# A transformer block on one core: the first 512 gate columns of the up projection are taken from rows without rstd and shift

## The chip, the cores and the metric

The kernel runs on one core of a Trainium2 chip. The metric is the device time of one execution in microseconds; before the change its median is 1419.35 us in three runs (1419.31 to 1419.57).

## What is computed

One layer of a diffusion backbone in fp32: 256 latent tokens and 256 context tokens of width D = 2048, neighbourhood attention (16 heads of 128), then a gated feed-forward part with a short convolution along the tokens (FFN_DIM 5504). Shift, scale and gate of both parts come from SiLU(c) @ w_ada. The part that the change touches:

```python
def rms_norm(x, g):
    y = x32 * lax.rsqrt(jnp.mean(x32 * x32, axis=-1, keepdims=True) + EPS)
    return (y * g).astype(x.dtype)

def modulate(x, shift, scale):
    return x * (1.0 + scale) + shift

def conv_ffn(h, w_up, conv_w, conv_b, w_down):
    gate, up = jnp.split(dwconv3(h @ w_up, conv_w, conv_b), 2, axis=-1)
    return (jax.nn.silu(gate) * up) @ w_down

x = x + g1 * y                                   # y: attention @ w_o
hf = modulate(rms_norm(x, norm_ffn_g[i]), sh2, sc2)
x = x + g2 * conv_ffn(hf, ...)
```

With gs2 = norm_ffn_g (1 + sc2), a row of hf is x gs2 rstd + sh2, where rstd is one number for each token.

## The kernel before

**Layout.** Features lie on the 128 partitions and tokens along a row, so x1 (the residual stream) is 16 row tiles (index kt or db) of 128 features by T = 256 tokens. The kernel has one long order of products on PE: the projection of q, k and v with the attention beside it, w_o, w_up, w_down.

**Split operands.** Each fp32 operand is split in two fp32r parts: hi, a rounded copy, and lo, the rest. A weight tile (128 rows by 2 row tiles by up to 512 columns) is loaded by `wload` on the SP queue into one of four wr buffers; `wpair` copies hi to wh on ACT (three buffers) and subtracts for lo on DVE into wl (two buffers, L158). A plan lists all tiles in order, and `ahead` keeps two split pairs ahead of use. The moving operand has hi and lo side by side: a row of 2T = 512 columns.

**`proj` (L709)** runs one piece of columns over all row tiles, two row tiles to a step: for each block of 128 columns and each row tile wh by the 512 columns (hi and lo; L723), then wl by the 256 hi columns (L729). At the end, columns 0 to 255 of a bank plus columns 256 to 511 are the result. With `fold` the 512 columns are taken as two products of 256 into the same bank columns, which need no addition later; the last piece of w_o (256 output features) is done so.

**The stage with w_o.** The table WO cuts the 2048 outputs into pieces: 768 in two halves of k, then 512, 512 and 256. After a piece each of its blocks db is added to x1 (L775, two operations, one if folded), squared on ACT for the sum over features (L780, added up by DVE in sacc2, L784), and multiplied by gs2 into `xg` on ACT (L785). Beside these products DVE accumulates the vectors g1, gs2 and sh2 from w_ada (L274), which `ada.tick` hands out after each step; `ada.drain` after the last but one piece finishes them (transposes on PE L282, reduction and addition on DVE L285, L288).

**Between w_o and w_up.** The squares of the last two blocks and sacc2 are summed over the partitions by six products with a column of ones (`col_sums`, L229). `rstd_rows` makes rstd of them (POOL power, three small DVE operations), a diagonal matrix (L215) and one product with ones (L220) that spreads rstd over all partitions; ACT copies it to rb2 (L222). Then for each row tile t = xg rb2 (on DVE, from the fourth on every second one on POOL), hf hi = t + sh2 (ACT, L814) and hf lo (DVE, L815). `hold` makes the weight splits that are emitted next wait for the last square and the diagonal.

**The stage with w_up.** The 5504 gate and 5504 up columns go in pieces of 512, gate and up in turn, so that a first pass takes gate columns 0 to 511 and a second the up columns 0 to 511. Beside a pass the finished four blocks of the pass before are handled in `side`: `drop` adds the two halves of a bank (L824, L825), `conv` the three taps, then `gate` or `up`.

**Order of the work.** The kernel is written engine-neutral; a scheduler with its own estimate of time puts each engine's instructions in an order. PE, DVE, ACT, POOL and SP each work through theirs.

## Time and profile before

| | |
|---|---|
| median of three runs | 1419.35 us (1419.31 to 1419.57) |
| the profiled execution | 1419.36 us |
| its span, first to last instruction | 1417.6 us |
| mean granted clock of PE | 0.996 |
| PE busy | 1386.8 us, 98% |
| DVE busy | 1022.4 us, 72% |
| ACT busy | 694.9 us, 49% |
| DMA | 317.13 MB, mean 224 GB/s |

All durations of the text come from the one profiled execution; its time is 0.01 us above the median. Between the span and the time lie 1.76 us of start and end. PE's matmuls are pipelined and their recorded ends are modelled, so a busy PE is best read by the distance of starts. A step's rhythm is such a distance.

### The profile page before, as it was taken

The page shows a single profiled execution, that of the slowest core. Times are in us where ns is not written, and L with a number is a line of the kernel's source. Part 1 is how long each engine was busy: PE and PEld are TensorE (multiplying, and loading weights), DVE is VectorE, ACT ScalarE, POOL GpSimd, SP SyncE. Part 2 cuts the span into 40 slices and gives each one's busy share as a digit, 9 for nine tenths or more (in the row PEclk, how much of TensorE's full clock was granted, in tenths as well). Part 3 has the DMA queues.
Part 4 walks back from the last instruction along what each step waited for, and adds up shares of the span by engine and source line. Part 5 has one row for each costly group of instructions (what it writes and reads, how often), then busy time and mean ns, then how long its engine had stood idle before and what let it go on. Part 6 is the DMA issues. An engine that isn't in the chain of part 4 may idle for free.

```text
span 1417.6 us, 20783 instructions
## 1 busy us (share of the span) xinstructions
PE 1386.8 (98%) x7608; PEld 1164.8 (82%) x7608; DVE 1022.4 (72%) x1669; ACT 694.9 (49%) x1212; POOL 59.9 (4%) x64
## 2 busy tenths in 40 slices
PE   4999999999999999999899999999999999999998
PEld 2566788888888888888788888888888888888888
DVE  4555678878877888788777888778787675545454
ACT  4322254564454564554565655556555554333343
POOL 1000010020010020000100000000000000000000
PEclk9999999999999999999899999999999999999999
DMA  9999637768776869475667777777776666666554
GB/s 304 357 353 292 223 104 237 227 214 257 233 238 192 276 201 291 157 250 178 225 187 237 237 236 238 225 237 235 231 230 189 175 192 197 188 200 201 169 181 154
DMA packets 208918, 317.13 MB, mean 224 GB/s; under 512 B 23360, under 2 KB 87744, under 8 KB 208816
## 3 DMA queue, kind: packets, MB, share of 16 engines
q1 hardware_dynamic: 208688, 315.79, 71.5%
q8 instruction: 59, 0.97, 0.3%
q14 instruction: 43, 0.35, 0.1%
q10 hardware_dynamic: 128, 0.01, 0.0%
HBM read 312.75 MB, written 3.01 MB: 223 GB/s over the span
## 4 chain that ended last, share of the span: by engine, by line
PE 94%; DMA 2%; DVE 2%; SPq 1%; ACT 1%; issue 1%; POOL 0%; DVEq 0%; ACTq 0%; POOLq 0%
PE pj L723 20%; PE pj L729 10%; PE mx L723 10%; PE pj L372 8%; PE pj L373 8%; PE pj L374 8%; PE ms L723 7%; PE mx L729 5%; PE ms L729 4%; PE mx L372 2%; PE mx L373 2%; PE ms L407 2%; PE mx L374 2%; DMA wx<-in_w_ada 1%; PE ms L627 1%; SPq L401 1%
## 5 line engine op out<-in xcount | busy, mean ns | idle before, releaser
L158 DVE TENSOR_TENSOR wl<-wr,wh 128x1024 fp32r<-128x1024 f32 (+2 forms) x425 | 478.1, 1126 | 284.8 <-PE pj L729 102.3
L157 ACT CAST wh<-wr 128x1024 fp32r<-128x1024 f32 (+2 forms) x425 | 412.6, 972 | 535.3 <-PE pj L723 164.3
L373 PE MATMUL pj<-wl,hh 128*128 128x512 f32 x512 | 202.7, 396 | 0.0
L374 PE MATMUL pj<-wh,hl 128*128 128x512 f32 x512 | 200.1, 393 | 0.0
L372 PE MATMUL pj<-wh,hh 128*128 128x512 f32 x512 | 193.0, 396 | 2.5 <-ACT hh L446 2.5
L274 DVE SCALAR_TENSOR_TENSOR acc<-wa,sT,acc 128x512 f32<-128x512 f32 x240 | 183.2, 765 | 2.5
L723 PE MATMUL pj<-hf,wh 128*128 128x512 f32 x688 | 176.1, 395 | 2.0 <-DVE hf L815 2.0
L723 PEld LDWEIGHTS pj<-hf,wh 128*128 128x128 f32 x688 | 124.6, 190 | 25.1 <-DVE hf L815 2.8
L372 PEld LDWEIGHTS pj<-wh,hh 128*128 128x128 f32 x512 | 95.7, 188 | 26.4 <-issue 3.4
L373 PEld LDWEIGHTS pj<-wl,hh 128*128 128x128 f32 x512 | 96.5, 188 | 21.5 <-DVE wl L158 0.9
L374 PEld LDWEIGHTS pj<-wh,hl 128*128 128x128 f32 x512 | 96.5, 188 | 18.8
L729 PEld LDWEIGHTS pj<-hf,wl 128*128 128x128 f32 x688 | 93.7, 190 | 6.7
L723 PE MATMUL mx<-hf,wh 128*128 128x512 f32 x352 | 97.7, 394 | 0.0
L729 PE MATMUL pj<-hf,wl 128*128 128x256 f32 x688 | 96.9, 283 | 0.0
L723 PE MATMUL ms<-hf,wh 128*128 128x512 f32 x336 | 90.9, 390 | 0.0
L723 PEld LDWEIGHTS ms<-hf,wh 128*128 128x128 f32 x336 | 63.1, 188 | 14.2
L474 DVE TENSOR_TENSOR vsum<-vsum,mx 128x512 f32<-128x512 f32 x64 | 43.1, 682 | 34.3 <-PE mx L374 34.1
L723 PEld LDWEIGHTS mx<-hf,wh 128*128 128x128 f32 x352 | 60.6, 190 | 7.8
L729 PEld LDWEIGHTS mx<-hf,wl 128*128 128x128 f32 x352 | 53.7, 189 | 6.8
L729 PE MATMUL mx<-hf,wl 128*128 128x256 f32 x352 | 55.9, 282 | 0.0
L729 PE MATMUL ms<-hf,wl 128*128 128x256 f32 x336 | 54.7, 283 | 0.0
L407 PE MATMUL ms<-wx,s 128*32 128x512 f32 (+1 forms) x288 | 36.9, 582 | 16.3 <-DMA wx<-in_w_ada 16.3
(248 smaller groups left out, 2029.6 us busy)
## 6 DMA issues: line engine op xcount, KB each, us to landing
wr<-in_w_up SPq DMA_DIRECT2D x160, 512.0 KB, 4.2
wa<-in_w_ada SPq DMA_DIRECT2D x128, 512.0 KB, 4.8
wr<-in_w_qkv SPq DMA_DIRECT2D x93, 512.0 KB, 4.2
wr<-in_w_down SPq DMA_DIRECT2D x63, 512.0 KB, 4.6
wx<-in_w_ada SPq DMA_DIRECT2D x56, 512.0 KB, 8.6
wr<-in_w_o SPq DMA_DIRECT2D x24, 512.0 KB, 5.0
wr<-in_w_down SPq DMA_DIRECT2D x45, 256.0 KB, 3.1
wr<-in_w_up SPq DMA_DIRECT2D x16, 384.0 KB, 3.4
```

Of the source, the lines that this page charges most:

```text
L157: a = nc.scalar.copy(hi[:, :kn, :cn], w[:, :kn, :cn])
L158: b = nc.vector.tensor_tensor(out=lo[:, :kn, :cn], in0=w[:, :kn, :cn], in1=hi[:, :kn, :cn].bitcast(F32), op=ALU.subtract,)
L274: nc.vector.scalar_tensor_tensor(out=acc, in0=w[:, k, :], scalar=s, in1=acc, op0=ALU.mult, op1=ALU.add)
L372: nc.tensor.matmul(pt, hh[:, kt, ts], wh[:, k, :], start=a, stop=False)
L373: nc.tensor.matmul(pt, hh[:, kt, ts], wl[:, k, :], start=False, stop=False)
L374: nc.tensor.matmul(pt, hl(kt, ts), wh[:, k, :], start=False, stop=z)
L401: load = nc.sync.dma_start(w.rearrange("p (k s f) -> p k s f", k=4, s=2)[:, :, which, :], w_ada[q * CH : (q + 1) * CH, c0 : c0 + n // 2].r ...
L407: nc.tensor.matmul(ap_[32 * k : 32 * k + 32, :n], s32[:, 4 * q + k, :], w[:, k * n : (k + 1) * n], start=(q == 0), stop=(q == 3), tile_pos ...
L474: nc.vector.tensor_add(acc[:, h0 + i, :], acc[:, h0 + i, :], pr_[i])
L627: nc.tensor.transpose(tp[:, kt * P : (kt + 1) * P], pr[:, kt * P : (kt + 1) * P], ident)
L723: nc.tensor.matmul(pts[b][:, : t1 - t0], wh[:, k, bs], mov(kt, slice(t0, t1)), start=(kt == 0 and t0 == 0), stop=False,)
L729: nc.tensor.matmul(pts[b][:, :T], wl[:, k, bs], mov(kt, slice(0, T)), start=False, stop=(kt == kn - 1),)
```

## The change

`proj` and its callers stay, but for the first gate piece the moving operand is another. The block's row x1 gs2 is itself split: ACT writes its hi part and a new DVE operation (L798 of the changed kernel) its lo part into `xgs`, two tiles of eight row tiles each, in rows of T + 2 = 258 columns; the last two columns hold sh2, also split. The first pass is run folded on these rows: per block and row tile three products of 258 columns (wh by hi, wh by lo, wl by hi). A bank then holds W x gs2 in 256 columns and W sh2 in the last two. `drop_late` finishes it: columns times rb2, plus the column of W sh2 as a bias. The 16 normalizations (`normalized`, now from x1, all on DVE and ACT) are handed out in `side` beside this first pass. `hold` goes. `act` creates its tiles when first used, since xgs lies in memory that they take later.

```diff
     def wpair(src, k0, kn, c0, cn):
...
-        with ExitStack() as order:
-            for ins in hold:
-                order.enter_context(tc.issue_after(ins))
-            a = nc.scalar.copy(hi[:, :kn, :cn], w[:, :kn, :cn])
...
             for b, bs, k in cells:
                 kt = k0 + k
-                for t0, t1 in ((0, T), (T, 2 * T)) if fold else ((0, 2 * T),):
+                for t in (slice(0, T), slice(T, 2 * T)) if fold else (slice(0, 2 * T),):
+                    m = mov(kt, t)
                     nc.tensor.matmul(
-                        pts[b][:, : t1 - t0], wh[:, k, bs], mov(kt, slice(t0, t1)),
-                        start=(kt == 0 and t0 == 0), stop=False,
+                        pts[b][:, : m.shape[-1]], wh[:, k, bs], m,
+                        start=(kt == 0 and t.start == 0), stop=False,
                     )
...
-    xg = big.tile([P, KD, T], F32, tag="row0", name="xg")
+    xgs = [
+        pool.tile([P, 8, 2, T + 2], F32R, tag=tag, name=f"xg_{tag}")
+        for pool, tag in ((big, "row1"), (hp, "hl1"))
+    ]
+
+    def xg(kt, part):
+        return xgs[kt // 8][:, kt % 8, part, :]
+
...
             ada.drain()
+            for j, x_ in enumerate(xgs):
+                sh = sh2T[:, 8 * j : 8 * j + 8].unsqueeze(2).to_broadcast([P, 8, 2])
+                nc.scalar.copy(x_[:, :, 0, T:], sh)
+                nc.vector.tensor_tensor(
+                    out=x_[:, :, 1, T:], in0=sh, in1=x_[:, :, 0, T:].bitcast(F32), op=ALU.subtract
+                )
...
-            nc.scalar.mul(xg[:, db, :], x1[:, db, :], gs2T[:, db : db + 1])
+            gs = gs2T[:, db : db + 1]
+            nc.scalar.activation(xg(db, 0)[:, :T], x1[:, db, :], AF.Copy, scale=gs)
+            nc.vector.scalar_tensor_tensor(
+                out=xg(db, 1)[:, :T], in0=x1[:, db, :], scalar=gs,
+                in1=xg(db, 0)[:, :T].bitcast(F32), op0=ALU.mult, op1=ALU.subtract,
+            )
...
-    hold[:] = [square.ins, diag]
+    rb2 = rstd_rows(fp, sums2, "y", nc.scalar.copy)[0]
...
-    for kt in range(KD):
+    def normalized(kt):
+
         t = fp.tile([P, T], F32, tag="t", name="t", bufs=3)
-        if kt > 2 and kt % 2:
-            nc.gpsimd.tensor_mul(t, xg[:, kt, :], rb2)
-        else:
-            nc.vector.tensor_mul(t, xg[:, kt, :], rb2p if kt < 2 else rb2)
+        nc.vector.scalar_tensor_tensor(
+            out=t, in0=x1[:, kt, :], scalar=gs2T[:, kt : kt + 1], in1=rb2,
+            op0=ALU.mult, op1=ALU.mult,
+        )
...
+    def drop_late(pt):
+
+        t = fp.tile([P, T], F32, tag="t", name="t", bufs=3)
+        z = fp.tile([P, T], F32, tag="z", name="z", bufs=4)
+        w = fp.tile([P, 1], F32, tag="w", name="w", bufs=2)
+        nc.scalar.copy(w, pt[:, T : T + 1])
+        nc.vector.tensor_mul(t, pt[:, :T], rb2)
+        nc.scalar.activation(z, t, AF.Identity, bias=w)
         return z
...
+            first = c1 == 0
+            if first:
+                side.extend([lambda kt=kt: normalized(kt) for kt in range(KD)])
+            pts = proj(
+                w_up, KD, c1, cn, xgv if first else hfv,
+                (lambda: side.tick(2.0)) if first else tick,
+                pts=[bank() for _ in range(4)][: cn // P], fold=first,
+            )
             side.drain()
```

What the scheduler makes of it, at the three places of which the prediction speaks. A row is line, operation, out<-in, shape of the output, count. The line numbers of the changed kernel differ: L723 is L721, L729 is L728, L158 is L155, L775 is L786, L784 is L795.

**PE, from the end of w_o into w_up.** om is the attention's output, wh and wl the weight parts, sacc and sq the sums of squares, yd the diagonal of rstd. Before:

```order
L723 MATMUL ms<-om,wh 128x256 x8
L729 MATMUL ms<-om,wl 128x256 x4
L229 MATMUL ms<-ones,sacc_5198 128x1 x2
L229 MATMUL ms<-ones,sq 128x1 x4
L220 MATMUL mx<-yd,ones 128x256
L723 MATMUL pj<-hf,wh 128x512 x8
L729 MATMUL pj<-hf,wl 128x256 x8
```

Now, from the end of w_o, and then the steps up to the diagonal:

```order
L728 MATMUL ms<-om,wl 128x256 x4
L721 MATMUL pj<-xg_row_5223,wh 128x258 x16
L728 MATMUL pj<-xg_row_5223,wl 128x258 x8
L721 MATMUL pj<-xg_row_5223,wh 128x258 x3
L226 MATMUL ms<-ones,sacc_5198 128x1 x2
L226 MATMUL ms<-ones,sq 128x1 x2
L721 MATMUL pj<-xg_row_5223,wh 128x258 x11
L226 MATMUL ms<-ones,sq 128x1 x2
L721 MATMUL pj<-xg_row_5223,wh 128x258 x2
```

```order
L728 MATMUL pj<-xg_row_5223,wl 128x258 x8
L721 MATMUL pj<-xg_row_5223,wh 128x258 x16
L728 MATMUL pj<-xg_row_5223,wl 128x258 x8
L721 MATMUL pj<-xg_row_5223,wh 128x258 x13
L217 MATMUL mx<-yd,ones 128x256
L721 MATMUL pj<-xg_row_5223,wh 128x258 x3
```

The sums moved from ahead of the first w_up product to behind 27 of them, the diagonal product into the fourth step, and every product of this pass has 258 columns.

**DVE, after the first six blocks of w_o.** x is x1, acc a w_ada accumulation, sacc the sum of squares. Before, and then now, from one wl to the next:

```order
L158 TENSOR_TENSOR wl<-wr,wh 128x1024
L272 TENSOR_SCALAR acc<-wa,sT 128x512
L775 SCALAR_TENSOR_TENSOR x_5196<-pj,g1T,x_5196 128x256
L775 SCALAR_TENSOR_TENSOR x_5196<-mx,g1T,x_5196 128x256
L784 TENSOR_TENSOR sacc_5198<-sacc_5198,sq 128x256
L775 SCALAR_TENSOR_TENSOR x_5196<-mx,g1T,x_5196 128x256
L158 TENSOR_TENSOR wl<-wr,wh 128x1024
```

```order
L155 TENSOR_TENSOR wl<-wr,wh 128x1024
L269 TENSOR_SCALAR acc<-wa,sT 128x512
L786 SCALAR_TENSOR_TENSOR x_5196<-pj,g1T,x_5196 128x256
L786 SCALAR_TENSOR_TENSOR x_5196<-mx,g1T,x_5196 128x256
L798 SCALAR_TENSOR_TENSOR xg_row_5223<-x_5196,gs2T,xg_row_5223 128x256
L795 TENSOR_TENSOR sacc_5198<-sacc_5198,sq 128x256
L798 SCALAR_TENSOR_TENSOR xg_row_5223<-x_5196,gs2T,xg_row_5223 128x256
L786 SCALAR_TENSOR_TENSOR x_5196<-mx,g1T,x_5196 128x256
L798 SCALAR_TENSOR_TENSOR xg_row_5223<-x_5196,gs2T,xg_row_5223 128x256
L155 TENSOR_TENSOR wl<-wr,wh 128x1024
```

Three of the new operations (L798) now stand between these two wl.

**DVE, beside the folded last piece of w_o.** Before, and then now, from the last w_ada reduction or the x1 operations to the fourth wl (the second wl is the first that is shown):

```order
L285 TENSOR_REDUCE sh2T<-ms 128x4
L288 TENSOR_TENSOR sh2T<-sh2T,sm 128x4
L775 SCALAR_TENSOR_TENSOR x_5196<-pj,g1T,x_5196 128x256 x2
L775 SCALAR_TENSOR_TENSOR x_5196<-mx,g1T,x_5196 128x256
L775 SCALAR_TENSOR_TENSOR x_5196<-pj,g1T,x_5196 128x256
L775 SCALAR_TENSOR_TENSOR x_5196<-mx,g1T,x_5196 128x256
L158 TENSOR_TENSOR wl<-wr,wh 128x2x256
L775 SCALAR_TENSOR_TENSOR x_5196<-pj,g1T,x_5196 128x256
L775 SCALAR_TENSOR_TENSOR x_5196<-mx,g1T,x_5196 128x256 x2
L784 TENSOR_TENSOR sacc_5198<-sacc_5198,sq 128x256
L158 TENSOR_TENSOR wl<-wr,wh 128x2x256 x2
```

```order
L786 SCALAR_TENSOR_TENSOR x_5196<-mx,g1T,x_5196 128x256
L155 TENSOR_TENSOR wl<-wr,wh 128x2x256
L786 SCALAR_TENSOR_TENSOR x_5196<-pj,g1T,x_5196 128x256
L282 TENSOR_REDUCE sh2T<-ms 128x4
L786 SCALAR_TENSOR_TENSOR x_5196<-mx,g1T,x_5196 128x256 x2
L795 TENSOR_TENSOR sacc_5198<-sacc_5198,sq 128x256
L798 SCALAR_TENSOR_TENSOR xg_hl_5224<-x_5196,gs2T,xg_hl_5224 128x256
L285 TENSOR_TENSOR sh2T<-sh2T,sm 128x4
L798 SCALAR_TENSOR_TENSOR xg_hl_5224<-x_5196,gs2T,xg_hl_5224 128x256
L155 TENSOR_TENSOR wl<-wr,wh 128x2x256
L795 TENSOR_TENSOR sacc_5198<-sacc_5198,sq 128x256
```

The reduction and addition for sh2T moved from ahead of the x1 operations to between the second and the third wl, and two new operations with them.

## Rows read from the trace of the kernel before

**Rows 1.** The head of the page: the span, and the line with each engine's busy time, its share of the span and its instructions (x).

```profile
span 1417.6 us, 20783 instructions
...
PE 1386.8 (98%) x7608; PEld 1164.8 (82%) x7608; DVE 1022.4 (72%) x1669; ACT 694.9 (49%) x1212; POOL 59.9 (4%) x64
```

**Rows 2.** The table by stretches: from and to in us, the length, then for PE, PEld, DVE, ACT and POOL the busy time and the count of instructions, then the granted clock of PE as a share of full speed, the share of the DMA engines, and GB/s.

```profile
625.00:630.00 5.00, 5.00 (x30) 4.24 (x29) 5.00 (x8) 4.24 (x8) 0.00 (x0) 1.00 0.66 192
650.00:655.00 5.00, 5.00 (x31) 4.41 (x30) 5.00 (x9) 1.92 (x3) 0.00 (x0) 1.00 0.62 217
665.10:676.57 11.47, 11.17 (x94) 10.97 (x93) 8.53 (x18) 6.55 (x14) 0.00 (x0) 1.00 0.53 163
677.16:686.35 9.19, 3.40 (x16) 2.38 (x14) 5.53 (x14) 4.85 (x10) 0.71 (x1) 0.65 0.89 303
686.35:691.10 4.75, 4.75 (x17) 3.98 (x18) 4.72 (x9) 2.98 (x7) 2.61 (x3) 0.61 0.71 262
691.10:710.90 19.80, 19.80 (x115) 17.41 (x114) 14.90 (x20) 11.82 (x17) 3.31 (x4) 1.00 0.56 164
710.90:733.30 22.40, 22.40 (x130) 19.70 (x129) 14.19 (x20) 14.14 (x22) 0.00 (x0) 1.00 0.65 188
```

**Rows 3.** The chain of work that ended last, from 664 to 712 us, in order of time: start, us, engine, tile and line, count. Lines that the text does not use are left out.

```profile
670.94 4.82 DMA wr<-in_w_up
...
678.17 0.41 DVE x L775
...
679.77 1.00 PE ms L229 x4
...
681.17 0.72 POOL yr L197
...
683.12 1.21 PE mx L220 x2
...
684.41 0.38 ACT yb L222
...
686.35 3.78 PE pj L723 x8
...
691.12 1.84 PE pj L723 x8
...
693.91 1.84 PE pj L723 x8
...
710.90 0.69 PE mx L723 x3
```

**Rows 4.** The timeline of PE, 667 to 678.5 us (the last piece of w_o, folded): start, us, engine, line, operation, out<-in, shape, count, and in brackets the idle time before it and what ended it.

```profile
669.39 0.74 PE L729 MATMUL ms<-om,wl 128*128 128x256 f32 x4 [0.30 <-DVE wl L158]
...
671.40 1.12 PE L723 MATMUL ms<-om,wh 128*128 128x256 f32 x8
672.36 0.64 PE L729 MATMUL ms<-om,wl 128*128 128x256 f32 x4
672.84 1.12 PE L723 MATMUL ms<-om,wh 128*128 128x256 f32 x8
...
676.68 0.64 PE L729 MATMUL ms<-om,wl 128*128 128x256 f32 x4
```

**Rows 5.** The same view of PE, 17 to 36 us (sums and the diagonal product of the first normalization, at full clock).

```profile
29.43 1.05 PE L229 MATMUL mx<-ones,sacc 128*128 128x1 f32 x8
...
33.05 0.70 PE L220 MATMUL mx<-cd,ones 128*128 128x256 f32 x2
```

**Rows 6.** The timelines of DVE (two rows) and of PE (one row), 622 to 627 us, after the first six blocks of w_o; columns as in rows 4.

```profile
622.53 1.21 DVE L158 TENSOR_TENSOR wl<-wr,wh 128x1024 fp32r<-128x1024 f32 x1
...
625.57 1.22 DVE L158 TENSOR_TENSOR wl<-wr,wh 128x1024 fp32r<-128x1024 f32 x1
...
626.93 0.65 PE L729 MATMUL ms<-om,wl 128*128 128x256 f32 x4
```

**Rows 7.** The timeline of DVE, 663 to 672 us, beside the folded piece of w_o; columns as in rows 4.

```profile
663.41 0.69 DVE L285 TENSOR_REDUCE sh2T<-ms 128x4 f32<-128x512 f32 x1 [0.61 <-PE ms L282]
...
664.58 0.88 DVE L775 SCALAR_TENSOR_TENSOR x<-pj,g1T,x 128x256 f32<-128x256 f32 x2 [0.28 <-PE pj L729]
665.37 0.47 DVE L775 SCALAR_TENSOR_TENSOR x<-mx,g1T,x 128x256 f32<-128x256 f32 x1
...
668.33 0.41 DVE L784 TENSOR_TENSOR sacc<-sacc,sq 128x256 f32<-128x256 f32 x1
668.66 1.28 DVE L158 TENSOR_TENSOR wl<-wr,wh 128x512 fp32r<-128x512 f32 x2
...
670.20 0.68 DVE L158 TENSOR_TENSOR wl<-wr,wh 128x512 fp32r<-128x512 f32 x1
```

**Rows 8.** Loads: the time from a DMA's issue to its landing of all loads into wr in 660 to 700 us, and the group of the w_ada loads in 640 to 720 us (count, KB each, median us to landing).

```profile
DMA to landing us min/median/max: 2.6/3.6/7.6
...
wa<-in_w_ada SPq DMA_DIRECT2D x4, 512.0 KB, 6.8
```

**Rows 9.** Groups of instructions by line and shape, 686 to 710.9 us (the first pass of w_up): line, engine, operation, out<-in, shapes, count | busy us, mean ns of one | idle time before them.

```profile
L815 DVE SCALAR_TENSOR_TENSOR hf<-t,sh2T,hf 128x256 fp32r<-128x256 f32 x16 | 10.4, 683 | 0.0
...
L158 DVE TENSOR_TENSOR wl<-wr,wh 128x1024 fp32r<-128x1024 f32 x7 | 8.5, 1216 | 3.2 <-PE pj L729 3.1
...
L810 POOL TENSOR_TENSOR t<-xg,yb 128x256 f32<-128x256 f32 x7 | 5.9, 846 | 11.6 <-DVE hf L815 11.6
```

More of the change, by code (lines that the diff above doesn't have):

```diff
@@ L145, in wload @@
         return w
-    last, hold = [], []
+    last = []
     def wpair(src, k0, kn, c0, cn):
@@ L153, in wpair @@
         lo = wp.tile([P, KT, CH], F32R, tag="wl", name="wl", bufs=2)
-        with ExitStack() as order:
-            for ins in hold:
-                order.enter_context(tc.issue_after(ins))
-            a = nc.scalar.copy(hi[:, :kn, :cn], w[:, :kn, :cn])
-            b = nc.vector.tensor_tensor(
-                out=lo[:, :kn, :cn], in0=w[:, :kn, :cn], in1=hi[:, :kn, :cn].bitcast(F32),
-                op=ALU.subtract,
-            )
+        a = nc.scalar.copy(hi[:, :kn, :cn], w[:, :kn, :cn])
+        b = nc.vector.tensor_tensor(
+            out=lo[:, :kn, :cn], in0=w[:, :kn, :cn], in1=hi[:, :kn, :cn].bitcast(F32),
+            op=ALU.subtract,
+        )
         last[:] = [a.ins, b.ins]
@@ L728, in proj @@
                 kt = k0 + k
+                m = mov(kt, slice(0, T))
                 nc.tensor.matmul(
-                    pts[b][:, :T], wl[:, k, bs], mov(kt, slice(0, T)), start=False,
-                    stop=(kt == kn - 1),
+                    pts[b][:, : m.shape[-1]], wl[:, k, bs], m, start=False, stop=(kt == kn - 1)
                 )
@@ L779, in block_kernel @@
             sq = row2k("sq")[:, :T] if db else sacc2
-            square = nc.scalar.activation(sq, x1[:, db, :], AF.Square)
+            nc.scalar.activation(sq, x1[:, db, :], AF.Square)
             if db >= KD - 2:
@@ L791, in block_kernel @@
     fp = ctx.enter_context(tc.tile_pool(name="fp", bufs=1))
-    rb2, rb2p, diag = rstd_rows(fp, sums2, "y", nc.scalar.copy)
-    hold[:] = [square.ins, diag]
+    rb2 = rstd_rows(fp, sums2, "y", nc.scalar.copy)[0]
     hf = hp.tile([P, KD, 2 * T], F32R, tag="hh", name="hf")
-    acts = [
-        pool.tile([P, 8, 2 * T], F32R, tag=tag, name=f"act_{tag}")
-        for pool, tag in ((big, "row0"), (big, "row1"), (hp, "hl1"))
-    ]
-    acts.append(fp.tile([P, KF - 24, 2 * T], F32R, name="act_fp"))
+    acts = {}
     def act(f, c):
         i = min(f // 8, 3)
+        if i not in acts:
+            pool, tag = ((big, "row0"), (big, "row1"), (hp, "hl1"), (fp, "act_fp"))[i]
+            n = KF - 24 if i == 3 else 8
+            acts[i] = pool.tile([P, n, 2 * T], F32R, tag=tag, name=f"act_{tag}")
         return acts[i][:, f - 8 * i, c]
-    for kt in range(KD):
+    def normalized(kt):
         t = fp.tile([P, T], F32, tag="t", name="t", bufs=3)
-        if kt > 2 and kt % 2:
-            nc.gpsimd.tensor_mul(t, xg[:, kt, :], rb2)
-        else:
-            nc.vector.tensor_mul(t, xg[:, kt, :], rb2p if kt < 2 else rb2)
+        nc.vector.scalar_tensor_tensor(
+            out=t, in0=x1[:, kt, :], scalar=gs2T[:, kt : kt + 1], in1=rb2,
+            op0=ALU.mult, op1=ALU.mult,
+        )
         sh = sh2T[:, kt : kt + 1]
@@ L825, in drop @@
         nc.vector.tensor_add(z, pt[:, :T], t)
+        return z
+    def drop_late(pt):
[5 more added lines that the diff above has]
+        nc.scalar.activation(z, t, AF.Identity, bias=w)
         return z
@@ L857, in up, with feature @@
         )
-    def feature(pt, f, fn, fc):
+    def feature(pt, f, fn, fc, drop):
         st = {}
@@ L879, in block_kernel @@
     hfv = lambda kt, c: hf[:, kt, c]
+    xgv = lambda kt, c: xg(kt, int(c.start > 0))
     for c0 in range(0, FF, CH):
@@ L884, in block_kernel @@
         for c1, fn, o in ((c0, gate, 0), (FF + c0, up, KF)):
-            pts = proj(w_up, KD, c1, cn, hfv, tick, pts=[bank() for _ in range(4)][: cn // P])
+            first = c1 == 0
[5 more added lines that the diff above has]
+                pts=[bank() for _ in range(4)][: cn // P], fold=first,
+            )
             side.drain()
@@ L889, in block_kernel @@
                 f = c0 // P + b
-                parts.append(feature(pt, f, fn, o + f))
+                parts.append(feature(pt, f, fn, o + f, drop_late if first else drop))
             for i in range(len(parts) + 2):
```

## The prediction

> **What bounds the kernel now.** The page's head comes first [rows 1]: TensorE is busy 98% of the span, so a change can only win where PE stands still or is slow, and it loses wherever PE has to wait once more. The table by stretches comes second [rows 2]. Here the reader is to see one hole, between the products with w_o and those with w_up: in the 9.19 us from 677.16 to 686.35 PE is busy 3.40 us, and the granted clock is 0.65 there and 0.61 in the stretch after it, a mix of its levels 1.2 and 2.4 GHz, against 1.00, all 2.4 GHz, in the others. The same table shows that VectorE (DVE) is busy for all of 625 to 630 and 650 to 655: in the stage with w_o it has no room. The chain of waits comes third [rows 3] and says what the hole is made of: the last two blocks of x1, their squares, the column sums on PE (to 680.77), the power on POOL, the diagonal product that spreads rstd over the rows (683.12), its copy on ScalarE (ACT), the first normalized rows, and at 686.35 the first product with w_up. The first step of that pass then takes 4.77 us (686.35 to 691.12), the next 2.79 (691.12 to 693.91), and the pass ends at 710.90.
>
> **What the change takes away.** The first 512 gate columns no longer wait for rstd. PE's order puts 27 of the new products right behind the last one with w_o and the sums only after those. Gone are the hole, 686.35 - 677.16 = 9.19 us; the excess of the first step, 4.77 - 2.79 = 1.98; and what the pass loses later, 710.90 - 691.12 - 7 x 2.79 = 0.25. The last w_o product starts at 676.68 as one of four at 0.12, hence 677.16 [rows 4]. Together 11.42 us.
>
> **What it adds on PE's own path.** (a) A step (two row tiles, four blocks) was eight products of 512 columns and eight of 256, 2.79 us; it becomes 24 of 258. The nearest row is the w_o piece that is folded in the same way, each product with its own weight load: twelve products of 256 from 671.40 to 672.84, 0.12 us each [rows 4]. So 24 x 0.12 x 258/256 = 2.90, and 8 x 0.11 = 0.9 us. Bounds: 0 from below (a 256 at half of a 512's pitch, 2.79/24 = 0.116 each); from above, a 258 that costs as much as a 512 (1.84/8 = 0.23, rows 3), 192 x 0.11 = 21 us. I take 0.9, as 258 lies two columns from 256. The Trainium skill, "TensorE: Matmul & The Clock Gate", section "Back-to-back issue gap", puts a warm product at N/2.4 + 2.5 ns. By that a step would go from 2.60 to 2.64 us, my estimate from that page, and the sum below would be 0.6 us better; the rows at 0.12 and 0.23 do not bear that formula out, and they decide.
>
> (b) The sums and the diagonal product lay in the hole and now stand among the products. Six sum products are 12 records. Eight of them took 1.05 us at full clock, one alone 0.25, so 0.114 each: 1.4 us. The diagonal's two records span 0.70, some 0.6 net [rows 5]. Together 2.0 us; at the hole's clock they cost 2.0 to 2.2 and 1.2 [rows 3], so the upper bound is 3.3.
>
> **What it adds on DVE in the stage with w_o.** Sixteen operations (x1 times gs2 minus its rounded part) of the shape of L775, for which two take 0.88 and one 0.47 (a successor starts some 0.08 before the recorded end), so 0.40 each [rows 7]: 6.4 us on a full engine. PE waits for DVE only through wl, so each wl is followed. (c1) After the first six blocks, three of these now stand ahead of the third wl: it ran from 625.57 to 626.79 and PE took it at 626.93 [rows 6]. With 1.2 us more it ends at 627.99, and PE stands 1.1 us. The next wl's have 1.1 us of room or more, as PE has moved too; about 0.1 more goes in the second group of blocks. (c2) In the folded last piece the third wl was already 0.30 us late for PE (669.39, rows 4). It is the first of two at 668.66 [rows 7]. The sh2T reduction (0.69) and its addition (0.16) now stand behind x1 instead of ahead of it, and with them two new operations: 0.6 + 0.1 + 0.8 = 1.5 us more between the second and the third wl. PE's transposes move behind the last 512-column group, so x1 starts 0.9 rather than 1.2 us later: 0.9 + 1.5 = 2.4. So PE's end of w_o slides from 677.16 to 679.56 in all. Bounds: 0 (only DVE work is added, so nothing below), and all of it, 6.4 + 0.7 = 7.1.
>
> (d) The first w_up tile is loaded when the fifth of eight folded wl frees a buffer. That ended at 670.88 (start 670.20, rows 7); the load took 4.82 us, and ACT's copy follows, so weights are there 6.0 us after it [rows 3]. Behind the third wl, which would end at 671.7, now stand two additions (0.33 each), two new operations, the shift columns (0.1) and two wl's (0.60, 0.68): the fifth ends near 674.5. Weights at 680.5 for a PE that is free at 679.56: 0.9 us. Bounds: 0, and 0.9 + 2.8 where the load lands after 7.6 instead of 4.8 us, the slowest near there [rows 8].
>
> **What is covered.** Normalizing moves beside the split products. DVE must there do 16 wl at 1.22 - 0.08 = 1.14 (18.2), 32 operations at 0.40 (12.8; the multiplication moves from POOL, where seven took 0.85 each, to DVE [rows 9]) and some 7 us of sums and convolutions, 38 us in two passes of 23.2 + 22.4 = 45.6; the row pair that the second pass needs first is done in the middle of the first. With no POOL beside, hf should take the 0.47 of L775, not 0.68 [rows 9]. If that cover fails, PE waits at the second pass. The rstd chain has some 3 us to spare: sums near 686, the diagonal ready near 689, and PE comes to it after four steps, near 692. On SP the four w_ada loads still wait for the sums; seven w_up loads instead of five stand ahead of them, and the eighth has until 702. The shift columns (two tiny operations twice), drop_late's four extra columns and act's lazy tiles: nothing, beside PE's work of the second pass.
>
> **Sum.** 11.42 - 0.9 - 2.0 - 2.4 - 0.9 = 5.2 us. The profiled execution took 1419.36 us, 0.01 above the median of the runs, so 1419.4 - 5.2 = **1414.2 us**. The first product with w_up would start near 680.5 and the first pass end near 705.7.
>
> **Rivals.** What a measurement of this kernel can tell from no change is about 0.2%, 2.8 us.
> A: the stage with w_o absorbs the new DVE work, since w_ada's accumulations can be put later; (c) and (d) vanish: 11.42 - 0.9 - 2.0 = 8.5, **1410.9**. For it: DVE is not full in the last piece (8.53 of 11.47 us, rows 2). Against it: 625 to 655 is full, and the third folded wl was late already. Chance 0.18.
> B: all DVE time lands on PE, 7.1 instead of 2.4: -0.5, **1418.9**. For it: PE and DVE are coupled there through two wl buffers. Against it: 3 of the 16 stand before no late wl. Chance 0.12.
> C: weights come late, because the hole was also the time in which the buffers filled (DMA share 0.89, 303 GB/s, rows 2). A step needs 512 KB in 2.9 us, 180 GB/s, but 2 MB of w_ada fall in the same stretch and are 6.8 us under way [rows 8]. One load slower by 2.8 us gives **1417.0**. Chance 0.08.
> D, slower: the split product of 258 columns has a price of its own, in all 192 of the first pass. Its rows are 1032 bytes apart and it crosses 256. The change loses from 0.12 + 5.2/192 = 0.147 us each; at a 512's 0.23 it is 1419.4 - 5.2 + 21 = **1435**. For it: no row has such a width. Against it: the 256-column rows. Chance 0.06.
> E: the sums or the diagonal hold PE in the pass as they did in the hole, so the change does not do what it says; PE's order has 27 products ahead of the first sum and 85 ahead of the diagonal, so only a chain over 10 us long could. About 1419. Chance 0.02.
>
> **How the numbers follow.** The forecast has 0.54. Faster by over 0.2% (below 1416.5): it and A, and a little of B and C, 0.73. Within: most of B, C and E, 0.20. Slower: D and a corner of B, 0.07. The range leaves out D, the upper third of B and the lower end of A: 1410.6 to 1418.2.
>
> **What would show it.** Right: the clock stays 1.00 from 665 to 735; products of 258 columns start some 0.9 us behind the last w_o product, at a pitch of 0.12; the end of w_o comes 2 to 3 us later than 677.16, with waits on wl after the first six blocks and in the folded piece; the diagonal product waits for nothing; the second pass takes 22.4 us. Wrong: a pitch above 0.147, a wait of PE on hf at the second pass, on wh from a load in the first, or no later end of w_o (then A).

## The result: 1424.8 us, slower than before by 0.4%

The changed kernel takes 1424.77 us in the median of six runs (1423.97 to 1427.04), the kernel before 1419.46 beside it (six runs, 1417.37 to 1421.05). The ratio is 1.0041, with a 95% interval of 1.0028 to 1.0053. The forecast of 1414.2 and its range up to 1418.2 are wrong, and so is the sign.

The head of the page of the changed kernel, to be held against [rows 1]:

```profile
span 1425.0 us, 20925 instructions
...
PE 1396.1 (98%) x7672; PEld 1166.4 (82%) x7672; DVE 1031.0 (72%) x1694; ACT 695.2 (49%) x1218; POOL 55.9 (4%) x57
```

PE is busy 9.3 us more than before, DVE 8.6. The stretches that answer to the hole and the passes of [rows 2], in the same columns: from the last w_o product to the first of 258 columns, the first pass, the second pass.

```profile
688.47:690.12 1.65, 0.16 (x2) 0.00 (x0) 0.02 (x1) 1.04 (x1) 0.00 (x0) 1.00 0.98 344
690.12:715.04 24.92, 24.92 (x206) 24.86 (x207) 20.24 (x36) 14.93 (x23) 0.71 (x1) 1.00 0.83 272
715.04:737.60 22.56, 22.56 (x127) 19.53 (x126) 19.96 (x35) 18.05 (x34) 0.00 (x0) 1.00 0.62 185
```

The hole of 9.19 us has become one of 1.65, the clock is 1.00 in all three, the first pass takes 24.92 us, the second 22.56. So what was to happen here happened. The timeline of PE in the same place (columns as in [rows 4]) shows the new order at work:

```profile
687.99 0.64 PE L728 MATMUL ms<-om,wl 128*128 128x256 f32 x4
690.12 2.17 PE L721 MATMUL pj<-xg_row,wh 128*128 128x258 f32 x16 [1.49 <-ACT wh L154]
...
693.45 0.50 PE L226 MATMUL ms<-ones,sacc 128*128 128x1 f32 x4
...
695.66 0.50 PE L226 MATMUL ms<-ones,sq 128*128 128x1 f32 x4
...
701.73 0.60 PE L217 MATMUL mx<-yd,ones 128*128 128x256 f32 x2
```

The first split product waits 1.49 us for its weights, the sums and the diagonal product run between the others, and neither the second piece of the sums (695.66) nor the diagonal (701.73) has a wait in brackets.

The loss is elsewhere. The view of one tile gives for each group of instructions the count, the shortest, median and longest duration in ns, and the start of the first and of the last one in us. For PE's products on the attention's output om and on the rows hf, before and then changed:

```profile
L723 PE MATMUL pj<-om,wh x128: 387/393/497, 576.7 to 662.5; 128*128 128x512 f32 x128
...
L723 PE MATMUL mx<-hf,wh x352: 389/395/398, 709.6 to 1169.0; 128*128 128x512 f32 x176
...
L723 PE MATMUL ms<-hf,wh x336: 389/389/395, 711.4 to 1169.5; 128*128 128x512 f32 x168
L729 PE MATMUL ms<-hf,wl x336: 283/283/283, 712.8 to 1171.7; 128*128 128x256 f32 x168
```

```profile
L721 PE MATMUL pj<-om,wh x128: 387/393/506, 585.2 to 672.9; 128*128 128x512 f32 x128
...
L721 PE MATMUL mx<-hf,wh x352: 390/393/405, 715.0 to 1176.3; 128*128 128x512 f32 x176
...
L721 PE MATMUL ms<-hf,wh x336: 390/395/405, 716.0 to 1176.7; 128*128 128x512 f32 x168
L728 PE MATMUL ms<-hf,wl x336: 278/282/288, 717.4 to 1178.9; 128*128 128x256 f32 x168
```

The first product with w_o starts at 585.2 instead of 576.7. Nothing that the change does comes ahead of it: 8.5 us are lost in the projections and the attention, which its diff does not touch. From there to the second pass (first ms<-hf,wh) it is 134.7 us before and 130.8 now, a gain of 3.9. From there to the last product on hf it is 460.3 and 462.9, a loss of 2.6; to the end of the span 245.9 and 246.1. So +8.5 - 3.9 + 2.6 + 0.2 = +7.4 us between the two spans of 1417.6 and 1425.0 (between the medians it is 5.3; the changed kernel's profiled execution, 1426.83 us, lies 2.1 above its median).

The rows before and after also say what kind of loss it is: a product of the same shape, ms<-hf,wh, has a median duration of 389 ns before and 395 now, with the clock at 1.00 in both. Not every group on hf is slower: mx<-hf,wh goes from 395 to 393. In the projections every group is:

```profile
L373 PE MATMUL pj<-wl,hh x487: 387/389/504, 99.8 to 573.2; 128*128 128x512 f32 x163
L372 PE MATMUL pj<-wh,hh x483: 387/389/504, 100.8 to 573.0; 128*128 128x512 f32 x161
...
L374 PE MATMUL pj<-wh,hl x487: 387/389/481, 100.1 to 573.4; 128*128 128x512 f32 x163
```

```profile
L370 PE MATMUL pj<-wl,hh x486: 387/393/505, 100.1 to 579.9; 128*128 128x512 f32 x162
L369 PE MATMUL pj<-wh,hh x482: 387/393/506, 100.7 to 579.7; 128*128 128x512 f32 x161
...
L371 PE MATMUL pj<-wh,hl x485: 387/393/485, 100.5 to 579.5; 128*128 128x512 f32 x162
```

The medians go from 389 to 393 ns. The distance from one start to the next, which counts for the time, goes from a median of 227 ns to 231 or 232 (table below).

### The profile page after: what moved, and what is told of

The parts are those of the page before. It is cut to its first block, busy times and chain, and to the rows that moved or that the text cites. A ratio compares the mean times of both kernels' runs of the same rounds, so it can differ in the third digit from the quotient of the medians.

```text
span 1425.0 us, 20925 instructions
## 1 busy us (share of the span) xinstructions
PE 1396.1 (98%) x7672; PEld 1166.4 (82%) x7672; DVE 1031.0 (72%) x1694; ACT 695.2 (49%) x1218; POOL 55.9 (4%) x57
## 4 chain that ended last, share of the span: by engine, by line
PE 94%; DMA 2%; DVE 2%; SPq 1%; ACT 0%; issue 0%; DVEq 0%; ACTq 0%
PE pj L721 20%; PE pj L728 10%; PE mx L721 9%; PE pj L369 8%; PE pj L370 8%; PE pj L371 8%; PE ms L721 7%; PE mx L728 5%; PE ms L728 4%; PE mx L369 2%; PE mx L370 2%; PE mx L371 2%; PE ms L404 2%; DMA wx<-in_w_ada 1%; PE ms L624 1%; SPq L398 1%
## 5 line engine op out<-in xcount | busy, mean ns | idle before, releaser
L155 DVE TENSOR_TENSOR wl<-wr,wh 128x1024 fp32r<-128x1024 f32 (+2 forms) x425 | 477.9, 1125 | 278.0 <-PE pj L728 100.7
L721 PE MATMUL pj<-hf,wh 128*128 128x512 f32 x624 | 159.8, 395 | 0.0
L721 PEld LDWEIGHTS pj<-hf,wh 128*128 128x128 f32 x624 | 111.9, 188 | 20.4
L721 PE MATMUL mx<-hf,wh 128*128 128x512 f32 x352 | 97.4, 394 | 0.0
L721 PE MATMUL ms<-hf,wh 128*128 128x512 f32 x336 | 92.7, 396 | 0.0
L728 PEld LDWEIGHTS pj<-hf,wl 128*128 128x128 f32 x624 | 84.6, 188 | 6.9
L728 PE MATMUL pj<-hf,wl 128*128 128x256 f32 x624 | 87.8, 283 | 0.0
L721 PEld LDWEIGHTS ms<-hf,wh 128*128 128x128 f32 x336 | 63.2, 188 | 14.9
L721 PEld LDWEIGHTS mx<-hf,wh 128*128 128x128 f32 x352 | 60.2, 188 | 7.8
L728 PEld LDWEIGHTS mx<-hf,wl 128*128 128x128 f32 x352 | 53.8, 188 | 8.0
L728 PE MATMUL mx<-hf,wl 128*128 128x256 f32 x352 | 56.0, 281 | 0.0
L728 PE MATMUL ms<-hf,wl 128*128 128x256 f32 x336 | 54.4, 282 | 0.0
L369 PE MATMUL mx<-wh,hh 128*128 128x512 f32 x128 | 53.2, 415 | 0.0
```

The lines of the kernel that those rows point to most:

```text
L155: b = nc.vector.tensor_tensor(out=lo[:, :kn, :cn], in0=w[:, :kn, :cn], in1=hi[:, :kn, :cn].bitcast(F32), op=ALU.subtract,)
L369: nc.tensor.matmul(pt, hh[:, kt, ts], wh[:, k, :], start=a, stop=False)
L721: nc.tensor.matmul(pts[b][:, : m.shape[-1]], wh[:, k, bs], m, start=(kt == 0 and t.start == 0), stop=False,)
L728: nc.tensor.matmul(pts[b][:, : m.shape[-1]], wl[:, k, bs], m, start=False, stop=(kt == kn - 1))
```

## What was suspected

Of the changed program only one thing reaches that far ahead: where its tiles lie. A row of xgs has 258 columns, so a tile of xgs is 8 x 2 x 258 x 4 = 16,512 bytes on each partition. It shares its place with earlier tiles of 16,384 (row1 and hl1), and the larger of them sets the room. So everything that is laid out behind row1 moves up by 128 bytes: hh and hl (the split rows of the projections), om, hf, and the third of the four tiles of activations; the fourth, act_fp, is now created later and lies elsewhere. The weights wh and wl lie ahead of it and stay. Before, hh lies at byte 74,944 of a partition, wh at 21,696 and wl at 33,984: hh is 208 x 256 bytes from wh and 160 x 256 from wl. Now 128 are added to both distances.

In a projection PE streams wh or wl against hh or hl, which it holds (the stationary operand); from w_o on it streams om and hf against wh and wl.

**T1**: the pace of a product depends on where its two operands lie. **T2**: the slower pace has another cause (the chip, the changed program's code). Beside them stands the question whether the forecast's own terms hold, above all (c), DVE's work in the stage with w_o.

## Experiments: is it the place?

All runs at a glance. The four columns behind the time are read from the same rows of the tile view as above, from each kernel's own profiled run; "start to w_o" is the start of the first product with w_o, which by itself differs by up to 2 us between runs of the same pace (576.5 to 578.6, 584.1 to 586.1). The last column is the median distance of starts in the projections, counted from the starts in the trace over some 480 to 575 pairs each: hh on wh to hh on wl, hh on wl to hl on wh, hl on wh to hh on wh.

| kernel | time, us (ratio to before, 95%) | start to w_o | w_o to second pass | to last product on hf | to the end | distances, ns |
|---|---|---|---|---|---|---|
| before | 1419.46 | 576.7 | 134.7 | 460.3 | 245.9 | 227, 227, 227 |
| changed | 1424.77 (1.0028 to 1.0053) | 585.2 | 130.8 | 462.9 | 246.1 | 231, 232, 231 |
| e0_after_again | 1425.88 (1.0023 to 1.0047) | 586.1 | 129.5 | 463.0 | 246.2 | 232, 232, 232 |
| e1_shift_rows | 1431.23 (1.0062 to 1.0088) | 584.1 | 136.2 | 463.0 | 247.7 | 232, 232, 231 |
| e2_same_places | 1412.72 (0.9933 to 0.9958) | 576.7 | 129.0 | 460.2 | 246.2 | 227, 227, 227 |
| e3_shift_all | 1421.09 (0.9994 to 1.0011) | 576.5 | 134.7 | 460.2 | 248.1 | 227, 227, 227 |
| f2_rows_256 | 1421.54 (0.9996 to 1.0014) | 578.4 | 133.9 | 460.2 | 247.0 | 227, 227, 227 |
| f3_hl_only | 1427.14 (1.0031 to 1.0059) | 584.0 | 134.5 | 460.3 | 247.3 | 227, 232, 234 |
| g1_row1_256 | 1413.36 (0.9936 to 0.9961) | 577.4 | 129.2 | 460.2 | 245.2 | 227, 227, 227 |
| g3_same_places_again | 1413.62 (0.9936 to 0.9961) | 577.4 | 128.9 | 460.2 | 245.6 | 227, 227, 227 |
| f4_act_fp | 1414.16 (0.9942 to 0.9967) | 578.6 | 129.3 | 460.2 | 245.2 | 227, 227, 227 |
| f6_no_lo | 1413.54 (0.9935 to 0.9965) | 578.6 | 127.3 | 460.3 | 245.3 | 227, 227, 227 |
| g2_pool_sum | 1414.33 (0.9943 to 0.9970) | 577.6 | 132.2 | 460.3 | 244.6 | 227, 227, 227 |

**e0_after_again**, the mark: the changed kernel once more, beside the next three on one chip.

> The changed kernel once more, beside the three runs below on the same chip. T1 (places): the change's own region, from the folded w_o columns to the first w_up pass, gains 4 to 5 us, and the rest of the program loses 9 to 10 us because the tiles of 16,512 bytes push the row tiles hh, hl and om, hf 128 bytes up; total 1424.8 us against 1419.5 before. T2 (the pace of the other stages differs for another reason, such as the chip's state or the program's code): the same total, so this run alone tells nothing apart; it is the mark that the others are read against.

It came at 1425.88, ratio 1.0035.

**e1_shift_rows**: the kernel before, and only the places that hh, hl, om and hf have in the changed one.

```diff
     hls = [hp.tile([P, KD // 2, 2 * T], F32R, tag=f"hl{i}", name=f"hl{i}") for i in range(2)]
+    padh = hp.tile([P, 32], F32, name="padh")
+    nc.gpsimd.memset(padh, 0.0)
...
     xc = big.tile([P, KD, T], F32, tag="row1", name="xc")
+    padb = big.tile([P, 32], F32, name="padb")
+    nc.gpsimd.memset(padb, 0.0)
```

> The kernel before, with nothing of the change but 128 bytes of padding in the two pools, so that hh, hl, om, hf and the tiles behind them lie exactly where the changed kernel has them. T1 (places): the 512-column products of the projections go from a median pitch of 227 ns to 231-232 ns, the attention and projection stage loses about 8 us by 590 us, the rest 1 to 3 us more, total 1428 to 1430 us. T2 (the pace differs for another reason): 227 ns stays, total 1419.5 us.

It is slower by 0.75%, 1431.23 us, 1.2 above the range expected. The tile view has the changed kernel's durations, in a program that is otherwise the one before:

```profile
L377 PE MATMUL pj<-wl,hh x486: 387/393/505, 99.7 to 579.4; 128*128 128x512 f32 x162
...
L727 PE MATMUL pj<-om,wh x128: 387/393/497, 584.1 to 670.3; 128*128 128x512 f32 x128
...
L727 PE MATMUL ms<-hf,wh x336: 390/395/404, 720.3 to 1181.1; 128*128 128x512 f32 x168
L733 PE MATMUL ms<-hf,wl x336: 279/281/287, 721.8 to 1183.3; 128*128 128x256 f32 x168
```

393 ns as in the changed kernel, w_o from 584.1, and 1183.3 - 720.3 = 463.0 us from the second pass to the last product on hf. T1 holds; a T2 in the code of the changed program is out, since this program has none of it.

**e2_same_places**: the other way round, the whole change and the old places.

```diff
     xgs = [
-        pool.tile([P, 8, 2, T + 2], F32R, tag=tag, name=f"xg_{tag}")
-        for pool, tag in ((big, "row1"), (hp, "hl1"))
+        pool.tile([P, n, 2, T + 2], F32R, tag=tag, name=f"xg_{tag}")
+        for pool, tag, n in ((big, "row1", 7), (hp, "hl1", 7), (big, "row0", 2))
     ]
...
```

> The changed kernel with the un-normalized rows split over three tiles of 7, 7 and 2 row tiles in place of two of 8, so that no tile grows beyond 16,384 bytes and hh, hl, om and hf lie where the kernel before has them; the change itself is whole. T1 (places): the projections' pitch is back at 227 ns and only the change's own region counts: 1413.5 to 1416.5 us, middle 1414.9. T2: 1424.8 us as the changed kernel.

It takes 1412.72 us, ratio 0.9945, and 1413.62 in a second set (**g3_same_places_again**, below): 8 and 7 us faster than before, a little under the lower end of what was expected. The same rows of the tile view, of e2:

```profile
L370 PE MATMUL pj<-wl,hh x487: 387/389/504, 99.7 to 573.1; 128*128 128x512 f32 x163
...
L721 PE MATMUL pj<-om,wh x128: 387/392/499, 576.7 to 663.9; 128*128 128x512 f32 x128
...
L721 PE MATMUL ms<-hf,wh x336: 387/389/397, 705.7 to 1163.7; 128*128 128x512 f32 x168
```

The durations are back at 389 ns and the first w_o product at 576.7, as before. So the change is a gain that its tiles' size turned into a loss.

**e3_shift_all**: weights and rows moved together.

```diff
+    padc = cp.tile([P, 32], F32, name="padc")
+    nc.gpsimd.memset(padc, 0.0)
     mhalf = cp.tile([P, 4], F32, name="mhalf")
```

> The kernel before with 128 bytes of padding ahead of all of it, so that the weight tiles and the row tiles move up by 128 bytes together. T1a (the distance between a product's weights and its rows counts): the distances are as before, 227 ns, total 1419.5 us. T1b (the place of the rows alone counts): 231-232 ns and 1428 to 1430 us. T2: 1419.5 us.

It is the same as before (0.9994 to 1.0011), with 227 ns. What counts is the distance of a product's two operands from each other (T1a), not where the rows lie.

**f2_rows_256**: the kernel before with 256 bytes ahead of hh, hl, om and hf, where e1 had 128.

```diff
     xc = big.tile([P, KD, T], F32, tag="row1", name="xc")
+    padb = big.tile([P, 64], F32, name="padb")
+    nc.gpsimd.memset(padb, 0.0)
```

> The kernel before with 256 bytes of padding ahead of hh, hl and all behind them; weights unmoved, so the distance of rows to weights is 256 bytes off its old value, modulo 512. T512 (the distance has to be a multiple of 512 bytes): the projections' median pitch is 230 ns or more, total 1427 to 1431 us. T256 (a multiple of 256 is enough, since the shifts seen so far were of 128): 227 ns and 1419.5 to 1421 us.

No difference to before (0.9996 to 1.0014), and 227 ns: with 256 bytes more the distance is as good as the old one.

**f3_hl_only**: 128 bytes between hh and hl.

```diff
     hh = hp.tile([P, KD, 2 * T], F32R, tag="hh", name="hh")
+    padh = hp.tile([P, 32], F32, name="padh")
+    nc.gpsimd.memset(padh, 0.0)
```

> The kernel before with 128 bytes of padding between hh and hl, so that in each three products of the projections (hh on wh, hh on wl, hl on wh) only the stationary operand hl is moved. T-load (what counts is the stream of one product beside the weight load of the next one): the product that runs ahead of an hl product, hh on wl, goes to a median pitch of 231 ns or more, and the other two stay at 227 ns. T-own (a product's own two operands count): hl on wh goes up and the other two stay. Either way about a third of the products, 2.5 to 4 us, total 1422 to 1425 us. If all three rise, neither holds.

It takes 1427.14 us, ratio 1.0045. The tile view of its projections (hh on wl, hh on wh, hl on wh):

```profile
L375 PE MATMUL pj<-wl,hh x486: 386/396/505, 100.9 to 579.1; 128*128 128x512 f32 x162
L374 PE MATMUL pj<-wh,hh x483: 388/390/505, 101.4 to 580.0; 128*128 128x512 f32 x161
...
L376 PE MATMUL pj<-wh,hl x486: 389/397/487, 101.2 to 579.6; 128*128 128x512 f32 x162
```

Neither theory holds alone. hh on wh stays at 390 ns; the product ahead of hl's (hh on wl, 396) and hl's own (397) both rise, in distances 232 and 234 against 227. So a product of the projections is slow when its own stationary operand or its successor's lies 128 bytes off the old distance from the rows that it streams. That two products of three pay fits a loss of 0.45% where one of three was expected to cost 0.2 to 0.3%. The rows hf are where they were, and the stretch of the products on hf has its 460.3 us. How the two operands come to disturb each other was not tried.

**g1_row1_256**: the smallest repair, two tiles as in the change, the first with rows of T + 4.

```diff
-        pool.tile([P, 8, 2, T + 2], F32R, tag=tag, name=f"xg_{tag}")
-        for pool, tag in ((big, "row1"), (hp, "hl1"))
+        pool.tile([P, 8, 2, T + w], F32R, tag=tag, name=f"xg_{tag}")
+        for pool, tag, w in ((big, "row1", 4), (hp, "hl1", 2))
...
-        return xgs[kt // 8][:, kt % 8, part, :]
+        return xgs[kt // 8][:, kt % 8, part, : T + 2]
...
```

> The changed kernel as it is, two tiles of 8 row tiles, but with rows of T+4 in place of T+2 in the first tile: it grows by 256 bytes instead of 128, so hh, hl, om and hf lie 256 bytes behind their old places, no longer 128. Nothing else differs. T1 (places; 256 was harmless in f2_rows_256): the projections' pitch is 227 ns and the total 1412 to 1415 us, about that of e2_same_places. If it is the tile's growth in itself, or the split into three tiles that helped e2_same_places: 1424.8 us and 231-232 ns.

1413.36 us, ratio 0.9948. It has two tiles, and the first grows even more than in the change; the 128 bytes were all that was wrong. e2 and g1 beat both kernels.

> e2_same_places once more, as the mark for the two beside it: 1412.7 to 1414.0 us.

The second set of e2 came at 1413.62, ratio 0.9949.

**f4_act_fp**: e2, and the last tile of activations brought to a multiple of 256 (here 512) bytes from the weights.

```diff
         if i not in acts:
+            if i == 3:
+                pada = fp.tile([P, 88], F32, name="pada")
+                nc.gpsimd.memset(pada, 0.0)
```

> The changed kernel with its places kept (three tiles of rows, as e2_same_places) and 352 bytes of padding ahead of the last tile of activations, act_fp, whose distance to the weights is then a multiple of 512 bytes; it was 160 off. T1 (places): the 228 products on act_fp go from a median of 234 ns to 227-231, which is 0.7 to 1.6 us; total 1411.1 to 1412.0 against 1412.7 of e2_same_places. T2: 234 ns stays.

The 152 products on it in the banks pj go from a median distance of 234 ns to 230, the 76 in mx from 234 to 233, less than expected, and 38 in ms that the expectation had not counted from 237 to 227. The time does not show it: 1414.16 us (ratio 0.9942 to 0.9967) against 1412.72 and 1413.62 of e2, where 1411.1 to 1412.0 was expected. From the last product on hf to the end it is 245.2 us; e2 had 246.2 and 245.6, g1, whose act_fp is not in line, 245.2 too. A gain of this size can't be told from no gain.

## Experiments: the forecast's term for DVE

**f6_no_lo**: e2 without the 16 low halves. A constant, written by POOL, takes their place.

```diff
+    for j, x_ in enumerate(xgs):
+        n = min(7, KD - 7 * j)
+        nc.gpsimd.tensor_copy(
+            x_[:, :, 1, :T], mhalf[:, 0:1].unsqueeze(2).to_broadcast([P, n, T])
+        )
...
-            nc.vector.scalar_tensor_tensor(
-                out=xg(db, 1)[:, :T], in0=x1[:, db, :], scalar=gs,
-                in1=xg(db, 0)[:, :T].bitcast(F32), op0=ALU.mult, op1=ALU.subtract,
-            )
```

> e2_same_places without the low halves of the un-normalized rows: a constant stands in their place, written on POOL, so that the 16 subtractions of 0.40 us are gone from DVE and all products stay. Theory of term (c) (DVE work ahead of the weight splits delays the w_o stage by 2.4 us): the waits on wl at the second step's piece (0.95 us), in the next (0.2) and in the folded piece (0.40 twice) shrink to 0.3 us or less in sum, the last w_o product ends 0 to 0.7 us after the 677.16 us of before instead of 2.4 after, and the total is 1410.5 to 1411.5. Rival (the delay is in the changed order of TensorE's own rows and in the transfers): w_o still ends about 2 us late and the total stays at 1412.7.

Partly. From the first w_o product to the second pass it takes 127.3 us, e2 129.0 and 128.9: 1.7 us went with the operations. Of e2's waits on wl behind the first six blocks (0.95) and in the folded piece (0.40 twice) only one of 0.42 is left. The expected end of w_o, within 0.7 us of before, did not come: the last group starts at 680.49, 101.9 us behind the first w_o product (578.57), where before has 99.9; but in this order seven of the split products stand ahead of that group. The time itself, 1413.54 us (0.9935 to 0.9965), is above the 1410.5 to 1411.5 expected and can't tell 1.7 us from e2's. One wait grew instead, the first on a wl in the stage (ms<-om,wl at 622.93), from 0.63 to 1.46 us. The timelines of POOL and DVE say why:

```profile
616.89 1.69 POOL L761 CAST xg_row<-mhalf 128x1792 fp32r<-128x1792 f32 x1 [32.48 <-PE ms L642]
```

```profile
613.59 0.69 DVE L155 TENSOR_TENSOR wl<-wr,wh 128x512 fp32r<-128x512 f32 x1 [0.95 <-PE pj L728]
...
617.61 1.51 DVE L155 TENSOR_TENSOR wl<-wr,wh 128x512 fp32r<-128x512 f32 x1
```

The same split of 512 columns takes 0.69 us alone and 1.51 beside POOL's copy. The experiment brought in a cost of its own, so what the operations cost by themselves is shown in part.

**g2_pool_sum**: f4 with the additions of squares on POOL.

```diff
-                nc.vector.tensor_add(sacc2, sacc2, sq)
+                nc.gpsimd.tensor_add(sacc2, sacc2, sq)
```

> f4_act_fp (places kept, act_fp aligned) with the adds of the squares (sacc2, 0.33 us each on DVE) moved to POOL. Theory of term (c): in the folded piece the splits of wl that TensorE waits for (0.40 us each) come 0.3 to 0.7 us sooner, w_o ends 0.5 to 1 us sooner than in f4_act_fp, and the total is about 1 us lower, 1411.0 to 1413.0. Rival: the two engines slow one another, DVE operations of 0.39 to 0.47 us get longer, and nothing is gained.

The rival. From the first w_o product to the second pass it takes 132.2 us, f4 129.3; the time is 1414.33 (0.9943 to 0.9970), against 1413.62 of g3 beside it. Half of the loss is one wait: after the first six blocks PE waits 2.37 us for wl (at 630.40), in f4 0.93 (at 629.85). Groups of DVE by line and shape in 620 to 682 us, columns as in [rows 9], first f4 and then g2; behind them the timelines of DVE and of POOL of g2, beside the folded piece of w_o:

```profile
L799 DVE SCALAR_TENSOR_TENSOR xg_hl<-x,gs2T,xg_hl 128x256 fp32r<-128x256 f32 x7 | 3.4, 488 | 0.0
```

```profile
L799 DVE SCALAR_TENSOR_TENSOR xg_hl<-x,gs2T,xg_hl 128x256 fp32r<-128x256 f32 x7 | 4.7, 680 | 0.0
```

```profile
673.83 0.68 DVE L155 TENSOR_TENSOR wl<-wr,wh 128x512 fp32r<-128x512 f32 x1
674.43 0.96 DVE L799 SCALAR_TENSOR_TENSOR xg_hl<-x,gs2T,xg_hl 128x256 fp32r<-128x256 f32 x1
675.31 1.23 DVE L155 TENSOR_TENSOR wl<-wr,wh 128x512 fp32r<-128x512 f32 x1
```

```profile
674.17 2.95 POOL L796 TENSOR_TENSOR sacc<-sacc,sq 128x256 f32<-128x256 f32 x3 [0.84 <-ACT sq L792]
```

While POOL adds, from 674.17 to 677.12, DVE's operations with two inputs in memory take about twice their time: xg_hl 0.96 us for 0.48, wl 1.23 for 0.68 just ahead. The Trainium skill says so: "SBUF — State Buffer", section "SBUF: two separate sides", has the two engines share a pair of ports, which an operation of DVE with two inputs in memory and one of POOL take from each other. This trace agrees. [rows 9] had shown it too: hf at 683 ns beside POOL's multiplications, and in the changed kernel, where POOL has none, 480:

```profile
L830 DVE SCALAR_TENSOR_TENSOR hf<-t,sh2T,hf 128x256 fp32r<-128x256 f32 x8 | 3.5, 480 | 0.4 <-ACT hf L829 0.4
```

## Why the prediction was wrong, step by step

**The step that failed** is one clause in "What is covered": "act's lazy tiles: nothing", and with it the sum's silent assumption that all stages outside the change keep their time. The lazy tiles themselves cost nothing; but the reason for them, that xgs lies in their places, was not followed to the size of xgs. 16,512 bytes where 16,384 had been moved hh, hl, om and hf by 128, and 8.5 + 2.6 us came on top, in stages that no term and no rival spoke of. e1 shows this cost by itself: 1431.2 us with none of the change's gain, 10.6 more than the kernel before beside it (1420.6). There was a sign in the trace of before that a product's pace is no constant of its shape: ms<-hf,wh at a median of 389 ns and mx<-hf,wh at 395, equal shapes at the same clock. It was not read.

**The local sum was right in sign and nearly in size.** At the old places the stretch from the first w_o product to the second pass takes 129.0, 128.9 and 129.2 us (e2, g3, g1) against 134.7, a gain of 5.5 to 5.8 where 5.2 was forecast. Whole, e2 (twice) and g1 come out at 1412.7 to 1413.6, inside the range given. By the medians e2's gain is larger, 7.9 us, than the 5.5 between the two spans (1417.6 and 1412.1): the trace of before is of an execution 1.25 us faster than the median beside e2 (1419.36 and 1420.61), that of e2 of one 1.16 slower than its own (1413.88 and 1412.72). Term by term, from e2's timelines of PE and (one row) of DVE, whose first w_o product starts at 576.7 as before:

```profile
627.91 0.74 PE L728 MATMUL ms<-om,wl 128*128 128x256 f32 x4 [0.95 <-DVE wl L155]
...
668.20 0.51 PE L728 MATMUL ms<-om,wl 128*128 128x256 f32 x2 [0.40 <-DVE wl L155]
...
671.03 0.69 DVE L155 TENSOR_TENSOR wl<-wr,wh 128x512 fp32r<-128x512 f32 x1
671.77 0.74 PE L728 MATMUL ms<-om,wl 128*128 128x256 f32 x4 [0.40 <-DVE wl L155]
...
679.07 0.64 PE L728 MATMUL ms<-om,wl 128*128 128x256 f32 x4
679.81 2.18 PE L721 MATMUL pj<-xg_row,wh 128*128 128x258 f32 x16
...
704.72 1.09 PE L721 MATMUL mx<-hf,wh 128*128 128x512 f32 x4
```

And from the timeline of the kernel before, its first w_up pass:

```profile
690.96 2.00 PE L723 MATMUL pj<-hf,wh 128*128 128x512 f32 x8
...
709.56 0.39 PE L723 MATMUL mx<-hf,wh 128*128 128x512 f32 x1
709.78 1.12 PE L729 MATMUL pj<-hf,wl 128*128 128x256 f32 x8
710.74 0.86 PE L723 MATMUL mx<-hf,wh 128*128 128x512 f32 x3
```

- What is removed (11.42): gone, at a clock of 1.00 throughout, but it was 11.0. The prediction read 691.12 and 710.90 from the chain, where a piece starts when the one before has ended. By PE's own starts the second step begins at 690.96, so the first step's excess is 1.82; and the pass ends at 710.74 with one product of the second pass already done in it (709.56 to 709.78), so that 710.74 - 0.22 - 690.96 - 7 x 2.79 leaves 0.03 for "what the pass loses later", not 0.25.
- (a) 0.9 for 192 products of 258 columns: the median distance is 0.120 us, and the last four steps, from 693.15 to 704.72, take 2.89 each where 2.90 was forecast, hence 0.8. Rival D (0.147 or more) is out. By the Trainium skill, "TensorE: Matmul & The Clock Gate", section "Back-to-back issue gap", N/2.4 + 2.5 ns gives an estimate of 0.110 us; the trace, at 0.120, does not bear that out.
- (b) 2.0 for sums and diagonal: the first pass takes 704.72 - 679.81 = 24.91 us; less eight steps of 2.89 that leaves 1.8.
- (c) 2.4 in the stage with w_o: the last group starts at 679.07 and w_o ends 0.48 later, at 679.55 instead of 677.16, so 2.39. The waits are where they were forecast: 0.95 after the first six blocks (1.1 forecast), 0.40 twice in the folded piece. There the third wl starts at 671.03 instead of 668.66 [rows 7], and PE takes it at 671.77 instead of 669.39 [rows 4], 2.38 later. In f6, without the operations, the stretch to the second pass is 1.7 shorter. Rival A (absorbed) and B (all of it lands) are both out.
- (d) 0.9 for the first w_up tile: 679.81 - 679.55 = 0.26 in e2, 1.65 in the changed kernel, from the same chain: the fifth split frees a buffer, the load follows. Only the load's own time differs, 5.39 us here and 4.00 in e2. In the changed kernel's chain, between its split, the load and ACT's copy:

```profile
682.87 0.61 DVE wl L155
...
683.53 5.39 DMA wr<-in_w_up
...
689.03 1.05 ACT wh L154
```

- The cover held: the second pass takes 22.38 us in e2 and 22.56 in the changed kernel (22.4 forecast), the chain for rstd has time to spare, and no wait on hf appears. Rivals C and E did not come to pass.

So 11.0 - 0.8 - 1.8 - 2.4 - 0.3 = 5.7 us, which is what the stretch gained. That 5.2 lies so near is in part luck: what is removed was put 0.4 too high, and the costs (a), (b) and (d) together 0.9 too high.

The mechanism that the change was made for is thus shown, and so is what hid it. What stays open is why two operands 128 bytes off disturb each other. The last stretch of the table, from the last product on hf to the end, varies between 244.6 and 248.1 us with no order by places. Most of that is one wait of PE for a weight tile in the products with w_down. It is 1.82 us in f3, 1.75 in e1 (ahead of mx<-act_row,wh at 1375.56), in f2 1.16, in e2 0.94, in e3 0.89, in the changed kernel 0.72; before and g2 have none above 0.15. In e3 the end after the last product is 1.3 us longer besides. Why that tile comes late in one run and not in another was not tried.
